# Gemv steps of the modulation on another engine around the first layer norm, and a table behind the last key activation

## The chip, the cores and the metric

One core of a Trainium2 chip runs the whole kernel in one launch. The metric is the device time of an execution in microseconds (us). An execution has five engines with a queue of instructions each: TensorE (PE, with its weight loads as PEld), VectorE (DVE), ScalarE (ACT), GpSimd (POOL) and SyncE (SP). SP issues nearly all transfers from memory. Each engine takes its instructions in a fixed order, and an instruction that waits holds up those behind it.

## The reference

All is fp32, with model width 2048, one sequence of 256 tokens, and weights of several hundred MB. Cut to what matters here:

```python
# two attention layers
for l in range(2):
    shift, scale, gate = split(silu(c) @ w_mod[l] + b_mod[l], 3)      # modulation: gemv
    h = x * (1 + scale) + shift
    if l == 0:
        y = diff_attention(h, ...)
    else:
        k, v, F = shared_kv(x, silu(c), w_kvmod, ...)   # hk = x*(1+scale')+shift'; hk @ w_kv
        y = forgetting_attention(h, w_q, w_out, k, v, F)
    x = layer_norm(ALPHA * x + gate * y, ln_g[l], ln_b[l])
# a state-space block
sh1, sc1, gt1, sh2, sc2, gt2 = split(silu(c2) @ w_mod2 + b_mod2, 6)   # gemv
h_ctx, h_lat = modulated rmsnorm of the context and of x
y = s5_mixer(h_ctx, h_lat, ...)      # linear recurrence over tokens, from the context's last state
x = x + gt1 * rmsnorm(y)
x = x + gt2 * rmsnorm(relu(modulate(rmsnorm(x), sh2, sc2) @ w1) ** 2 @ w2)
```

The modulation vectors are products of one activated vector with a wide matrix. They depend on no token, so they can be computed at any time before their use; what they cost is the reading of their weights and a pass of some engine over them.

## The kernel before

**Layout.** Activations lie transposed: `x` (tile `xres`) is 16 tiles of 128 features by 256 tokens. Each big product is done in three reduced-precision matmuls: a weight `w` is split into `wh` (cast by ScalarE, line 133) and `wl = w - wh` (VectorE, line 134), an activation likewise into H and L; then `hH*wh + hL*wh + hH*wl` (lines 162 to 164) are added in PSUM.

**The stream of weights.** `weights()` delivers the next block of 128 output features (1 MB in two loads). Each call also does two things in passing: one step of a background gemv, `bg()`, and as many steps of a side job, `step()`, as the cycle `steps` says.

**The background gemv.** `gemv()` works a modulation vector off in two halves of eight steps each. A step loads two 128x1024 tiles `graw` of 512 KB each from SP's queue; their pool `rg` has four buffers and is shared with the tile `wc` of the context. The step is used one call later (`LATE = 1`), in one of two ways. On "pe" it is eight matmuls, which the trace shows as 16 (an fp32 matmul shows as two), that add into a PSUM tile `g` (line 221). On "dve" it is two instructions `gacc += graw * c` (line 236). A half that has had a "dve" step is `open` until it is closed with matmuls of `gacc`. Which engine a step gets is a cycle of names set for each stage by `policy()`: `P_ON0` in the output projection of layer 0, `P_KV` in the keys' and values' stage, `P_QG` in the attention stage, `P_ON1` in the output projection of layer 1; `None` means no step. The jobs are done in the order of `JOBS`. The job `mc` has two outputs and runs on TensorE whatever the policy says. No step is ever dropped, so what one stage leaves out a later one has to do.

**The stages around the change.** `out_norm(0)` ends layer 0: 16 output blocks, the sums of the layer norm by matmuls, a chain of small VectorE instructions with an inverse root (`rsqrt`, lines 325 to 333), a broadcast of mean and root by TensorE (`lnb`, line 342), and then `norm(j)`: two VectorE instructions for each of 16 tiles (lines 1109 and 1110). `layer1()` makes the keys' activations from it: `affine_split` (lines 416 to 419) runs `norm(j)`, scales and casts on ScalarE (`u`, `kH`) and subtracts on VectorE (`kL`). The keys' stage then has 16 blocks (`mm_t`), the values' stage 16 half blocks (`mm_n`); the forget gate is computed behind the first block. A generator `s5_outputs_table` (`vgen`), with instructions on VectorE, ScalarE and TensorE and loads and stores on SP and POOL, is a side job of these 32 calls. The attention stage follows (32 calls), with the generator `ctx_states` as side job as soon as `mc` is done: it computes the state that the context leaves, in eight blocks of six levels each (lines 1332 to 1335). It runs on in `out_norm(1)`. `s5_mix` starts with the lines

```python
1364        self.bg_use(0)
1365        while self.open:
1366            self.bg(1, "dve")
1367            self.bg_use(0)
```

and then normalizes, modulates and transposes the tiles for the scan (lines 1407 to 1409), which is VectorE's.

**What sets the order.** The program is written in the order above, but a scheduler places each instruction on its engine's queue by a simulated timeline; the buffers of the pools set what a load has to wait for. `issue_after(ins)` is an extra edge that holds instructions behind `ins` on `ins`'s own engine, here VectorE; instructions on other engines are not held by it.

## Time and profile before

| | us |
|---|---|
| median of three timed executions | 2538.9 (2536.18 to 2539.73) |
| the profiled execution | 2539.89 |
| its span, first to last instruction | 2538.1 |
| TensorE busy | 2363.0 |
| VectorE busy | 1748.6 |
| ScalarE busy | 1191.3 |

The mean granted clock of TensorE is 0.953 of full speed. The durations further down are those of the profiled execution; its own time is 1.8 us more than its span, and 1.0 us more than the median. Names like `gacc<-graw` say what an instruction writes and reads. Times in the timeline count from the span's start.

### The profile page before, as it was taken

The numbers are of one execution on the slowest core, as the hardware profiler recorded it, in microseconds if no ns is written. First come the engines' busy times: TensorE is split into PE (matmuls) and PEld (weight loads), VectorE is DVE, ScalarE is ACT, GpSimd is POOL, SyncE is SP. The second block draws the span as 40 slices with busy tenths as digits, with TensorE's granted clock in tenths as the row PEclk, the third lists the DMA queues.
The fourth block names the chain that finished last, engine by engine and source line by source line (L and its number), as shares of the span: only waits on it lengthen the run. The fifth ranks groups of instructions, "written<-read, shape, count | busy, mean of one in ns | idle before, by whom it ended". The sixth has DMA issues, their size and how long they took to land.

```text
span 2538.1 us, 49977 instructions
## 1 busy us (share of the span) xinstructions
PE 2363.0 (93%) x19934; PEld 2042.3 (80%) x19934; DVE 1748.6 (69%) x3369; ACT 1191.3 (47%) x2069; POOL 96.4 (4%) x213
## 2 busy tenths in 40 slices
PE   5699999999989999999998569999899999999997
PEld 1289999999678888888896457898688888888885
DVE  3288778877785555788787896775864665665655
ACT  0455454445355556555443443544544443443442
POOL 0000000000001111000000000000000000000000
PEclk8599999999979999999998779999899999999998
DMA  9999999888869998888786357995356655556552
GB/s 324 337 337 321 323 328 340 304 286 300 281 210 346 327 338 295 286 273 295 235 295 245 116 182 271 359 318 194 117 186 192 189 189 189 185 188 190 189 185 94
DMA packets 195450, 644.78 MB, mean 254 GB/s; under 512 B 32624, under 2 KB 41072, under 8 KB 194832
## 3 DMA queue, kind: packets, MB, share of 16 engines
q1 hardware_dynamic: 187744, 620.47, 71.5%
q0 software_dynamic: 7472, 21.11, 2.1%
q8 instruction: 156, 2.56, 0.4%
q14 instruction: 78, 0.64, 0.1%
HBM read 615.80 MB, written 25.69 MB: 253 GB/s over the span
## 4 chain that ended last, share of the span: by engine, by line
PE 50%; issue 34%; DVE 7%; DMA 7%; ACT 2%; SPq 0%; POOL 0%; DVEq 0%; ACTq 0%; POOLq 0%
PE pj L162 10%; PE pj L163 10%; PE pj L164 10%; DMA graw<-in_w_mod 5%; PE g L221 3%; PE pjv L199 3%; PE pjv L200 2%; PE pjv L201 2%; PE ko L1451 2%; DVE scan_t L1407 1%; DVE S L1409 1%; DVE scan_t L1408 1%; PE y L1480 1%; PE st L369 1%; DVE gacc L236 1%
## 5 line engine op out<-in xcount | busy, mean ns | idle before, releaser
L134 DVE TENSOR_TENSOR wl<-w,wh 128x1024 fp32r<-128x1024 f32 x631 | 769.7, 1223 | 486.4 <-ACT wh L133 475.5
L133 ACT CAST wh<-w 128x1024 fp32r<-128x1024 f32 x632 | 658.1, 1048 | 741.0 <-PE pj L175 281.0
L175 PE MATMUL pj<-h,wh 128*128 128x512 f32 x1024 | 362.1, 399 | 5.7 <-DVE h L419 3.8
L175 PE MATMUL pj<-d,wh 128*128 128x512 f32 x1024 | 358.6, 396 | 0.0
L176 PE MATMUL pj<-h,wl 128*128 128x256 f32 x1024 | 287.0, 280 | 1.1 <-DVE wl L134 1.1
L176 PE MATMUL pj<-d,wl 128*128 128x256 f32 x1024 | 284.8, 279 | 0.0
L236 DVE SCALAR_TENSOR_TENSOR gacc<-graw,csilu,gacc 128x1024 f32<-128x1024 f32 x200 | 255.8, 1279 | 36.3 <-DMA graw<-in_w_mod 31.5
L175 PEld LDWEIGHTS pj<-h,wh 128*128 128x128 f32 x1024 | 193.6, 189 | 54.0 <-issue 3.9
L175 PEld LDWEIGHTS pj<-d,wh 128*128 128x128 f32 x1024 | 191.9, 188 | 47.5 <-PE pj L176 1.7
L162 PE MATMUL pj<-hH,wh 128*128 128x256 f32 x768 | 221.5, 289 | 5.2 <-ACT hH L418 4.0
L164 PE MATMUL pj<-hH,wl 128*128 128x256 f32 x768 | 221.4, 289 | 0.5 <-DVE wl L134 0.5
L163 PE MATMUL pj<-hL,wh 128*128 128x256 f32 x768 | 221.0, 288 | 0.0
L221 PE MATMUL g<-graw,czc 128*32 128x256 f32 x1840 | 169.5, 452 | 42.7 <-DMA graw<-in_w_mod 39.1
L176 PEld LDWEIGHTS pj<-h,wl 128*128 128x128 f32 x1024 | 194.2, 190 | 1.5 <-DVE wl L134 1.5
L176 PEld LDWEIGHTS pj<-d,wl 128*128 128x128 f32 x1024 | 192.8, 188 | 0.4
L162 PEld LDWEIGHTS pj<-hH,wh 128*128 128x128 f32 x768 | 148.8, 194 | 8.8 <-ACT hH L418 4.1
L164 PEld LDWEIGHTS pj<-hH,wl 128*128 128x128 f32 x768 | 148.5, 194 | 4.5 <-issue 3.3
L163 PEld LDWEIGHTS pj<-hL,wh 128*128 128x128 f32 x768 | 148.8, 194 | 3.8 <-issue 3.7
L162 PE MATMUL pj<-h1H,wh 128*128 128x256 f32 x512 | 146.3, 288 | 0.0
L163 PE MATMUL pj<-h1L,wh 128*128 128x256 f32 x512 | 145.9, 286 | 0.0
L164 PE MATMUL pj<-h1H,wl 128*128 128x256 f32 x512 | 145.1, 284 | 0.0
L221 PEld LDWEIGHTS g<-graw,czc 128*32 128x32 f32 x1840 | 48.8, 117 | 115.7 <-DMA graw<-in_w_mod 88.4
(475 smaller groups left out, 5067.6 us busy)
## 6 DMA issues: line engine op xcount, KB each, us to landing
graw<-in_w_mod SPq DMA_DIRECT2D x384, 512.0 KB, 5.8
w<-in_mlp_in SPq DMA_DIRECT2D x128, 512.0 KB, 3.7
w<-in_mlp_out SPq DMA_DIRECT2D x128, 512.0 KB, 3.7
w<-in_a_in SPq DMA_DIRECT2D x96, 512.0 KB, 6.1
graw<-in_w_kvmod SPq DMA_DIRECT2D x64, 512.0 KB, 6.0
w<-in_b_in SPq DMA_DIRECT2D x64, 512.0 KB, 5.6
w<-in_glu SPq DMA_DIRECT2D x56, 512.0 KB, 5.6
w<-in_a_v SPq DMA_DIRECT2D x32, 512.0 KB, 5.8
```

Of the source, the lines that this page charges most:

```text
L133: nc.scalar.copy(h, src)
L134: (eng or (nc.gpsimd if next(self.spl) else nc.vector)).tensor_sub(l, src, h)
L162: self.nc.tensor.matmul(ps, h, aH, start=kt == order[0] and not opened, stop=False)
L163: self.nc.tensor.matmul(ps, h, aL, start=False, stop=False)
L164: self.nc.tensor.matmul(ps, l, aH, start=False, stop=kt == order[-1] and last)
L175: self.nc.tensor.matmul(ps, h, view(aH, 0, [[T, 2], [1, T]]), start=kt == order[0], stop=False)
L176: self.nc.tensor.matmul(ps[:, 0], l, aH, start=False, stop=kt == order[-1])
L199: self.nc.tensor.matmul(ps[:, i], aH[:, s], h, start=half == 0 and i == 0 and k == 0, stop=False)
L200: self.nc.tensor.matmul(ps[:, i], aH[:, s], l, start=False, stop=False)
L201: self.nc.tensor.matmul(ps[:, i], aL[:, s], h, start=False, stop=half == 1 and i == 1 and k == 7)
L221: nc.tensor.matmul(st["g"][32 * q:32 * q + 32], self.cz[c][:, ch * 2 + s], raw[s][:, q * 256:q * 256 + 256], start=st["n"] == 0, stop=ch = ...
L236: nc.vector.scalar_tensor_tensor(acc, raw[s], cc, acc, op0=MUL, op1=ADD)
```

## The change

Five things. (1) `P_ON0` gives no gemv step in the last four of the 16 output blocks of layer 0: 9 steps rather than 12. (2) The six steps at the start of layer 1 are issued ahead of `affine_split` rather than behind it, and on TensorE; before they took the engine that the job's table names, VectorE. (3) `affine_split` returns its last subtraction, and the VectorE instructions of every side job are held behind that one until the end of the values' stage. (4) `vgen` starts at the second call, and every eighth call does two of its steps. (5) `P_KV` begins with TensorE.

```diff
--- before.py
+++ after.py
@@ -50,12 +50,13 @@
 KO_K = 12
 P_START = ("pe",)
 P_L0A = ('dve', 'pe')
-P_KV = ('dve', 'pe')
+P_KV = ('pe', 'dve')
+P_VT = (1, 1, 1, 1, 1, 1, 1, 2)
 P_QG = ('dve', 'dve', 'pe')
 P_W = ("pe",)
 P_GLU = ('dve',)
 P_MLP = ('dve', None, None)
-P_ON0 = ('dve', 'dve', 'dve', None)
+P_ON0 = ('dve', 'dve', 'dve', None) * 3 + (None,) * 4
 P_ON1 = ('pe', 'dve', None)
 BG_V = 2
 BG_W = 0
@@ -271,8 +272,9 @@
 
     def step(self):
 
-        while self.side and next(self.side[0], True):
-            self.side.pop(0)
+        with self.tc.issue_after(self.after) if self.after else nullcontext():
+            while self.side and next(self.side[0], True):
+                self.side.pop(0)
 
     def flush(self, job):
         while job in self.side:
@@ -416,7 +418,8 @@
             nc.scalar.activation(u, src(j), AF.Identity, scale=S[:, j:j + 1], bias=B[:, j:j + 1])
             aH, aL = dst(j)
             nc.scalar.copy(aH, u)
-            nc.vector.tensor_sub(aL, u, aH)
+            last = nc.vector.tensor_sub(aL, u, aH).ins
+        return last
 
     def pair(self, name):
         H, L = self.act_tile(F32R, name + "H"), self.act_tile(F32R, name + "L")
@@ -728,6 +731,7 @@
             self.steps = itertools.cycle((1,))
             self.open = False
             self.side = []
+            self.after = None
             self.x = xr.tile([128, KT, T], F32, name="xres")
             mod = lambda n: self.vt.tile([128, KT], F32, name=n)
             self.m0 = [mod(f"m0_{i}") for i in range(3)]
@@ -1119,8 +1123,8 @@
             self.bg_finish(n)
         S, B = self.small_bg("lk", V("lg0"), self.mk[1], V("lb0"), self.mk[0])
         k_ = self.pair("k")
-        self.affine_split(self.norm, S, B, k_)
-        self.bg(BG_K, E_K)
+        self.bg(BG_K, "pe")
+        self.after = self.affine_split(self.norm, S, B, k_)
         Fs = self.cp.tile([48, T], F32R, name="Fs")
         nid = self.cp.tile([48, 16], F32R, name="nid")
         FT = self.cp.tile([128, 2, 16], F32, name="FT")
@@ -1168,9 +1172,10 @@
         kT, v = [], []
         self.policy(P_KV, X_KV)
         vgen = self.s5_outputs_table(self.act.tile([128, 4096], F32, name="gen2_ws", tag="act"))
-        self.side.append(vgen)
         for j in range(32):
             if j == 1:
+                self.side.append(vgen)
+                self.steps = itertools.cycle(P_VT)
                 F = forget()
             if j == 3:
                 forget_t(F)
@@ -1189,6 +1194,8 @@
                         nc.scalar.copy(t, ps[:, :, h * 128:h * 128 + 128])
                         v.append(t)
         self.flush(vgen)
+        self.steps = itertools.cycle((1,))
+        self.after = None
         for i in (1, 0):
             self.bg_finish(f"m1_{i}")
         s1 = self.plus1("s1_1", self.m1[1])
```

Counted over the whole program, TensorE has 56 gemv matmuls more and VectorE 14 gacc instructions fewer; everything else is there as often as before. The lines of the changed kernel are up to seven higher than those of the kernel before (line 236 becomes 237, 419 becomes 421, 1109 and 1110 become 1113 and 1114).

By the stages, the gemv's steps come to stand as follows: start of layer 1, 6 on VectorE before, 6 on TensorE now; keys and values, 3 on VectorE and 29 on TensorE before, 4 and 28 now; attention, 18 and 14 before, 16 and 16 now; output projection of layer 1, 11 both times; the loop at the start of `s5_mix`, 3 before, 6 now, all on VectorE. `ctx_states` begins one head later.

VectorE's queue among the first keys, before. `gacc` is the gemv, `vprod` and `gen_ws` are the table, the other three the norm and the keys:

```order
L1110 TENSOR_TENSOR xres<-xres,lnb 128x256
L1109 TENSOR_TENSOR xres<-xres,lnb 128x256
L419 TENSOR_TENSOR kL<-u,kH 128x256
L236 SCALAR_TENSOR_TENSOR gacc<-graw,csilu,gacc 128x1024
L1110 TENSOR_TENSOR xres<-xres,lnb 128x256
L1109 TENSOR_TENSOR xres<-xres,lnb 128x256
L419 TENSOR_TENSOR kL<-u,kH 128x256
L553 TENSOR_TENSOR vprod<-gen_ws 128x512
L554 TENSOR_TENSOR vprod<-gen_ws 128x512
L236 SCALAR_TENSOR_TENSOR gacc<-graw,csilu,gacc 128x1024
L1110 TENSOR_TENSOR xres<-xres,lnb 128x256
L1109 TENSOR_TENSOR xres<-xres,lnb 128x256
```

The same place now:

```order
L421 TENSOR_TENSOR kL<-u,kH 128x256
L1114 TENSOR_TENSOR xres<-xres,lnb 128x256
L1113 TENSOR_TENSOR xres<-xres,lnb 128x256
L421 TENSOR_TENSOR kL<-u,kH 128x256
L1114 TENSOR_TENSOR xres<-xres,lnb 128x256
L1113 TENSOR_TENSOR xres<-xres,lnb 128x256
L421 TENSOR_TENSOR kL<-u,kH 128x256
L1114 TENSOR_TENSOR xres<-xres,lnb 128x256
L1113 TENSOR_TENSOR xres<-xres,lnb 128x256
L421 TENSOR_TENSOR kL<-u,kH 128x256
L1114 TENSOR_TENSOR xres<-xres,lnb 128x256
L1113 TENSOR_TENSOR xres<-xres,lnb 128x256
```

The gemv's and the table's instructions have left this stretch; the three instructions of a key tile follow each other.

VectorE's queue at the end of the norm's first inverse root and behind it, at the start of `s5_mix`, before. `ry` and `rq` are the root, `rc` leads to the second root (the rms norm's):

```order
L1093 COPY mr1_16129<-ry_16136 128x2
L1102 TENSOR_TENSOR rc_16153<-rc_16153,ry_16136 128x2
L1103 SCALAR_TENSOR_TENSOR rc_16153<-ra_16152,rc_16153 128x2
L1104 TENSOR_TENSOR rc_16153<-rc_16153,ry_16136 128x2
L1105 TENSOR_SCALAR rc_16153<-rc_16153,ms_14546 128x2
L236 SCALAR_TENSOR_TENSOR gacc_15739<-graw_16242,csilu_147,gacc_15739 128x1024
L1106 TENSOR_SCALAR rc_16153<-rc_16153 128x2
L1109 TENSOR_TENSOR xres_99<-xres_99,lnb_16147 128x256
L325 TENSOR_SCALAR ry_16163<-rc_16153 128x2
L1110 TENSOR_TENSOR xres_99<-xres_99,lnb_16147 128x256
L1109 TENSOR_TENSOR xres_99<-xres_99,lnb_16147 128x256
L327 TENSOR_TENSOR rq_16164<-ry_16163 128x2
```

A piece of the same chain now, between the sums and the first root; `ctx_ws` is the last block of the context's states:

```order
L237 SCALAR_TENSOR_TENSOR gacc_15989<-graw_16258,csilu_147,gacc_15989 128x1024
L1342 TENSOR_TENSOR ctx_ws_12029<-ctx_ws_12029 128x16x32
L327 TENSOR_SCALAR ry_16115<-lv_16111 128x2
L237 SCALAR_TENSOR_TENSOR gacc_15989<-graw_16260,csilu_147,gacc_15989 128x1024
L1339 TENSOR_TENSOR ctx_ws_12029<-ctx_ws_12029 128x512
L1340 TENSOR_TENSOR ctx_ws_12029<-ctx_ws_12029 128x512
L329 TENSOR_TENSOR rq_16116<-ry_16115 128x2
L1102 SCALAR_TENSOR_TENSOR ra_16131<-sums_16105,mr1_16108 128x2
L1341 TENSOR_TENSOR ctx_ws_12029<-ctx_ws_12029 128x512
L237 SCALAR_TENSOR_TENSOR gacc_15989<-graw_16264,csilu_147,gacc_15989 128x1024
L330 SCALAR_TENSOR_TENSOR rq_16116<-rq_16116,lv_16111 128x2
L1103 SCALAR_TENSOR_TENSOR rc_16132<-lq_16110,ms_14483,ra_16131 128x2
```

Before, one `gacc` stands between the sums and the second root, and now there are eleven, with the context's 512-element instructions between them.

TensorE's queue at the end of the same norm, before. `st` and `sums` are the norm's sums, `lnb` the broadcast of mean and root; the broadcast `rb` of the second root comes two rows further on:

```order
L221 MATMUL g_15549<-graw_16037,czc2_154 32x256 x4
L221 MATMUL g_15549<-graw_16039,czc2_154 32x256 x4
L369 MATMUL st_15403<-zsq_16104,mw_14538 3x256
L369 MATMUL st_15403<-xres_99,mw_14538 3x256
L369 MATMUL st_15403<-zsq_16109,mw_14538 3x256
L369 MATMUL st_15403<-xres_99,mw_14538 3x256
L369 MATMUL st_15403<-zsq_16114,mw_14538 3x256
L369 MATMUL st_15403<-xres_99,mw_14538 3x256
L369 MATMUL st_15403<-zsq_16119,mw_14538 3x256
L364 MATMUL st_15403<-zero_137 128x256
L379 MATMUL sums_16126<-sel_ln_160,sumst_16123 128x6 x2
L342 MATMUL lnb_16147<-idn_130,mr1_16129 128x128 x4
```

And now:

```order
L371 MATMUL st_15375<-zsq_16098,mw_14475 3x256
L366 MATMUL st_15375<-zero_137 128x256
L698 MATMUL inc_16155<-uctx_15395,wc_16028 64x64
L698 MATMUL inc_16156<-uctx_15395,wc_16028 64x64 x2
L381 MATMUL sums_16105<-sel_ln_160,sumst_16102 128x6 x2
L344 MATMUL lnb_16126<-idn_130,mr1_16108 128x128 x4
L344 MATMUL rb_16152<-idn_130,ry_16142 128x128 x2
L222 MATMUL g_16243<-graw_15985,czc2_154 32x256 x4
L222 MATMUL g_16243<-graw_15987,czc2_154 32x256 x4
L246 MATMUL g_16243<-gacc_15989,one32_139 32x256 x4
```

The gemv matmuls of the half step on TensorE stood ahead of the sums, and stand now behind `rb`. Until they have run, their two `graw` buffers of four are not free.

## Rows read from the trace of the kernel before

**Rows 1.** The page, busy time and share of the span by engine.
```profile
PE 2363.0 (93%) x19934; PEld 2042.3 (80%) x19934; DVE 1748.6 (69%) x3369; ACT 1191.3 (47%) x2069; POOL 96.4 (4%) x213
```

**Rows 2.** Windows by stage: us, busy us (instructions) per engine, clock, DMA share, GB/s.
```profile
686.00:735.00 49.00, 35.88 (x175) 29.23 (x176) 44.23 (x92) 24.89 (x51) 2.50 (x8) 0.65 0.66 210
735.00:965.00 230.00, 230.00 (x2404) 200.29 (x2406) 134.35 (x189) 127.62 (x242) 38.82 (x86) 1.00 0.92 321
...
985.00:1240.00 255.00, 251.61 (x2572) 224.17 (x2571) 196.28 (x340) 141.86 (x295) 5.97 (x12) 1.00 0.84 287
...
1352.00:1375.00 23.00, 21.96 (x226) 16.59 (x224) 17.32 (x39) 5.42 (x14) 0.00 (x0) 1.00 0.90 334
1375.00:1490.00 115.00, 60.75 (x1448) 48.45 (x1450) 106.81 (x550) 52.32 (x111) 1.39 (x4) 0.70 0.40 139
```

**Rows 3.** Timeline of VectorE, 685 to 702: start, us, instruction.
```profile
693.29 1.28 DVE L236 SCALAR_TENSOR_TENSOR gacc<-graw,csilu,gacc 128x1024 f32<-128x1024 f32 x1
694.50 0.15 DVE L1089 TENSOR_TENSOR lq<-mr 128x2 f32<-128x2 f32 x1
...
698.14 0.42 DVE L1109 TENSOR_TENSOR xres<-xres,lnb 128x256 f32<-128x256 f32 x1 [1.31 <-PE lnb L342]
```

**Rows 4.** VectorE's groups, 698 to 738: shapes, count, busy us, mean ns, idle.
```profile
L236 DVE SCALAR_TENSOR_TENSOR gacc<-graw,csilu,gacc 128x1024 f32<-128x1024 f32 x7 | 8.9, 1275 | 0.0
...
L134 DVE TENSOR_TENSOR wl<-w,wh 128x1024 fp32r<-128x1024 f32 x4 | 4.9, 1217 | 0.0
L553 DVE TENSOR_TENSOR vprod<-gen_ws 128x512 f32<-128x512 f32 x4 | 2.7, 681 | 0.0
```

**Rows 5.** Tile kL: duration in ns (min/median/max), first and last start.
```profile
L419 DVE TENSOR_TENSOR kL<-u,kH x16: 414/415/425, 701.1 to 734.6; 128x256 fp32r<-128x256 f32 x16
```

**Rows 6.** TensorE's groups, 698 to 738.
```profile
L163 PE MATMUL pj<-kL,wh 128*128 128x256 f32 x54 | 19.8, 374 | 4.8 <-DVE kL L419 4.8
L164 PE MATMUL pj<-kH,wl 128*128 128x256 f32 x52 | 18.2, 355 | 1.2 <-DVE wl L134 1.2
L162 PE MATMUL pj<-kH,wh 128*128 128x256 f32 x55 | 15.7, 359 | 2.9 <-ACT kH L418 2.9
```

**Rows 7.** Windows within the ramp.
```profile
698.00:706.00 8.00, 5.51 (x22) 4.70 (x21) 7.83 (x17) 4.22 (x10) 0.00 (x0) 0.50 0.77 234
...
710.00:723.00 13.00, 10.48 (x45) 9.39 (x45) 13.00 (x27) 6.76 (x13) 0.55 (x1) 0.50 0.63 198
```

**Rows 8.** Timeline of TensorE, 740 to 748.
```profile
745.18 0.28 PE L164 MATMUL pj<-kH,wl 128*128 128x256 f32 x1
745.30 0.28 PE L162 MATMUL pj<-kH,wh 128*128 128x256 f32 x1
...
745.75 1.07 PE L221 MATMUL g<-graw,czc 128*32 128x256 f32 x16
```

**Rows 9.** Timeline of VectorE, 1350 to 1408.
```profile
1357.83 0.68 DVE L1333 TENSOR_TENSOR ctx_ws<-ctx_ws 128x512 f32<-128x512 f32 x1
...
1362.01 1.28 DVE L236 SCALAR_TENSOR_TENSOR gacc<-graw,csilu,gacc 128x1024 f32<-128x1024 f32 x1 [2.16 <-DMA graw<-in_w_mod]
...
1374.22 0.16 DVE L1087 TENSOR_SCALAR mr<-sums 128x2 f32<-128x2 f32 x1 [0.37 <-PE sums L379]
...
1378.08 1.28 DVE L236 SCALAR_TENSOR_TENSOR gacc<-graw,csilu,gacc 128x1024 f32<-128x1024 f32 x1
...
1381.89 0.16 DVE L333 SCALAR_TENSOR_TENSOR ry<-rq,ry 128x2 f32<-128x2 f32 x1
...
1406.41 0.23 DVE L1408 TENSOR_TENSOR scan_t<-scan_t,S 128x64 f32<-128x64 f32 x1
```

**Rows 10.** DMA issues, 700 to 725: count, KB, median us to landing.
```profile
graw<-in_w_mod SPq DMA_DIRECT2D x7, 512.0 KB, 3.9
```

**Rows 11.** DMA issues, 1370 to 1392.
```profile
graw<-in_w_mod SPq DMA_DIRECT2D x5, 512.0 KB, 8.6
```

## The prediction

> **What bounds the kernel now.** I read the page's first section, then busy time by stage, and, for the two stages that the change reaches, the timelines of VectorE and TensorE. TensorE is busy for 93% of the span and VectorE for 69% [rows 1], but these are averages. By stage [rows 2] the reader is to see that TensorE is full in the keys' and values' stage (230.0 of 230 us at full clock) and in the attention stage (251.61 of 255), so that there a VectorE instruction costs nothing and a TensorE instruction its whole length. Two stretches are VectorE's. One is the ramp behind the first layer norm, 686 to 735: VectorE 44.23 of 49, TensorE 35.88 at a mean clock of 0.65. The other begins at 1375: VectorE 106.81 of 115, TensorE 60.75. The change lightens the first and, as the order of the instructions tells, loads the head of the second.
>
> **The ramp (place A): what is taken away.** From the first norm instruction at 698.14 [rows 3] to the end of the last kL at 734.6 + 0.41 = 735.0 [rows 5], VectorE works 36.9 us almost without a gap. Consecutive instructions overlap a little: the gacc at 693.29 is 1.28 long and the next row starts 1.21 behind it. So I price each by its length less 0.08: 0.335 us for kL (0.415 [rows 5]) and for the two norm instructions of the same size, 1.2 for gacc, 1.14 for a wl split, 0.6 for a 512-element table instruction [rows 4]. 48 x 0.335 = 16.1 for the norm and the keys, 7 x 1.2 = 8.4 for gacc, 4 x 1.14 = 4.6 for the weights, and 12 table instructions, of which one group of four is shown, 7.2. The sum is 36.3, which agrees with 36.9. In the changed order six of the seven gaccs are gone from there and the table stands behind the last kL: 16.1 + 1.2 + 4.6 = 21.9 us, 15 less.
>
> The statistics of the norm, ahead of it, also hold a gacc: it runs at 693.29 and the chain goes on only at 694.50 [rows 3]. Without it, and with the gaccs ahead of the sums gone too, I take 1 to 2.3 us off the start, so the first norm at about 696.5 and the last kL at 718 to 719, some 16 us earlier.
>
> **The ramp: what TensorE makes of it.** TensorE runs 54 + 52 + 55 = 161 matmuls of the keys between 698 and 738 [rows 6]; at the pitch of full clock (0.12 us, the first two of [rows 8]) they are 19.3 us. So it loses 40 - 19.3 = 20 us there: 8.9 waiting for kL, kH and wl, the first key's kH among them [rows 6], and the rest by the clock. The granted clock was 0.50, 1.2 GHz, from 698 to 706 with TensorE busy 5.51 of 8, and 0.50 again from 710 to 723 [rows 7]. After the change a kL comes every 21.9 / 16 = 1.4 us rather than 2.3, so TensorE has more to do at a stretch. It also has six gemv steps, of which three stand before the first key matmul and three among them; a step is 16 matmuls, 1.07 us at full clock [rows 8]. I take: start of key matmuls at 698; 19.3 of matmuls; 3 us of gemv steps behind the start; 3 us for the stretch that still runs at half clock; 0.5 idle: 723.8 against 738, a gain of 14. The bounds are 6 and 15: at 6 most of the ramp stays at 1.2 GHz (twice the pitch on 161 matmuls costs 19 more in full, and the 21.9 us in which the keys come hide more than half of it), at 15 TensorE follows VectorE without a loss. Above 16 there is no room, since kL itself comes no earlier.
>
> **Place A, the smaller parts.** The steps of the first modulation in the keys' stage now begin with TensorE, and 28 gemv steps in the stage run there rather than 29: -1 us. Three steps less in the out-projection (9 for 12): VectorE isn't what binds there, 0. The table moves later in a stage where VectorE has 134.35 of 230 [rows 2]; that hides it. If its tail reaches beyond the stage it stands among the first activations of the attention stage: 0 to +3, taken 1. The attention stage takes 16 TensorE steps for 14, in a stage where TensorE is full: +2. Sum of A: -14 - 1 + 1 + 2 = -12, with ends -2 and -14.
>
> **Start of S5 (place B): what is added.** Since three steps fewer were done early, and no step was taken away in all, three more are left when the out-projection of layer 1 ends. There the code finishes whatever half is open on VectorE: before 3 steps were left (6 loads of 512 KB), now 6 (12 loads), each with a gacc of 1.28 us. The state table of the context also starts one head later and ends later. On VectorE's order all this stands inside the two inverse roots of the second norm, on which S5 waits. Before, from the first instruction of the statistics at 1374.22 to the end of the second root at 1381.89 + 0.16 = 1382.05, there are 7.8 us, with one gacc (1378.08) [rows 9]. Now the order has 11 gaccs and the last block of the context's table in that chain: 10 more gaccs at 1.2 are 12.0; 8 table instructions of 512 elements at 0.68 - 0.08 (the row at 1357.83) are 4.8; four of 256 at 0.33 and eleven smaller ones add 2.4, less some 2 us of the short latencies that these hide. That is 17 more, by VectorE's own work alone, from the moment when the sums arrive.
>
> **Place B: the loads.** Four buffers take the loads. Two of them hold the half step that TensorE will do, and on TensorE's order it now stands behind the instruction that waits for the second root. So the twelve loads go through two buffers: a load is issued when the gacc before it on its buffer has ended. From issue to landing a graw took 3.9 us in the ramp with few others [rows 10] and 8.6 at 1370 to 1392, where many were in flight [rows 11]; before, VectorE waited 2.16 us for one at 1362.01 [rows 9]. Two loads each 3.9 + 1.28 = 5.2 us, six rounds, are 31 us; the first is issued at about 1370, so the last gacc ends at 1401 to 1402, and the second root some 1.5 us behind it, 1403: +21. By VectorE's work alone it would be 1375 + 25 = 1400: +18. The Trainium skill (DMA: Bandwidth & Descriptors, Anatomy of one DMA — SWDGE (gpsimd) path) gives a fit of 2.0 us plus bytes over 436 GB/s, 3.2 us for such a load, measured on another path; by it six rounds are 27 and VectorE's work would decide, +18. No run here shows 3.2. I take +20; nothing behind it makes up for it, since VectorE is at 106.81 of 115 from 1375 to 1490 [rows 2]; the scan begins at 1406.41 [rows 9] and shifts with it. Ends: +10 (the last waits of the old order, up to 5 us before the scan, take part, and the first gaccs fall before the sums) and +25 (loads at 5 to 6 us).
>
> **The sum.** -12 + 20 = +8. The profiled execution took 2539.89 us, so 2547.9; the median of the timed runs stands 1.0 below it, at 2538.9, and so 2547.
>
> **The rivals.**
> - *Only the added work counts at S5's start, and the ramp pays in full.* If the loads land early and VectorE does most gaccs before the sums, the added work is six gaccs (7.2) and some of the table (2.4), less the 5.7 us that VectorE stands idle from 1352 to 1375 (17.32 of 23 busy [rows 2]): +4. With -14 for A: 2538.9 - 10 = 2529. The idle time speaks for it; against it that VectorE's order is fixed, with eleven gaccs behind the sums, and that two of four buffers are held. It decides if the second root ends within some 15 us of the sums, where it was 7.8. Chance 0.13; not slower.
> - *The two places cancel.* The ramp gives its utmost (A -14), S5's start costs 13 to 15: 2539. Each end is within its bounds. Chance 0.18.
> - *TensorE stays at half clock.* The gemv matmuls now stand among the keys' matmuls, and they need loads; where one is late the array idles and the clock stays at 0.50 as it did from 710 to 723. The ramp gives only 6 (A -4), S5's start costs 20: 2555. For it: the clock fell before after a single wait; against it: the loads are issued in the out-projection. Chance 0.14.
> - *The table isn't held where it is meant to be.* The edge is on VectorE's queue alone, so its ScalarE copies and SP loads run early and could stand before keys' work: 1 or 2 us of the gain. That is 2549, and its chance is in the forecast's.
>
> **How the numbers follow.** The forecast with +1 to +13 has 0.55; the others as given. What a measurement of this kernel can tell from no change is 0.2%, 5.1 us. Slower by more: 0.85 of 0.55, and 0.14, together 0.61. Same: 0.15 of 0.55 and 0.9 of 0.18, 0.24. Faster: the rest, 0.15. The range runs from 2530, which takes in most of the first rival, to 2558, which takes in the half clock. The likeliest case's own is 2540 to 2554.
>
> **What would show it.** Right: VectorE from the first norm to the last kL in 22 to 24 us, without gacc but one, and TensorE past its 161 matmuls 12 to 15 us sooner; eleven gaccs between the statistics of the second norm and its second root, with waits for graw; the scan's first row about 20 us late against the same point of the ramp. Wrong: the second root within 15 us of the sums, or a clock of 0.50 through the ramp.

## The result and the profile after

| us | before | after |
|---|---|---|
| median of four timed executions | 2539.3 (2536.2 to 2541.7) | 2560.9 (2556.1 to 2565.0) |
| the profiled execution, its span | 2539.9, 2538.1 | 2559.4, 2557.6 |

The ratio is 1.0083, with an interval of 1.0068 to 1.0098: slower, by more than twice what was forecast. The marks below are differences of the first or last start of a tile (`sums`, `kL`, `h1L`, `scan_t`, `xy`, the last being the result of the gated unit behind the scan). They divide the span, so the last column adds up to the 19.5 us that the span has grown.

| from one mark to the next, us | before | after | change |
|---|---|---|---|
| start to the first norm's sums | 692.2 | 688.8 | -3.4 |
| to the last key matmul | 149.7 | 137.0 | -12.7 |
| to the last value matmul | 122.3 | 122.4 | +0.1 |
| to the first attention matmul | 2.2 | 3.9 | +1.7 |
| to the last attention matmul | 269.7 | 281.7 | +12.0 |
| to the second norm's sums | 137.8 | 138.3 | +0.5 |
| to the scan's first row | 32.5 | 55.5 | +23.0 |
| to the end of the span | 1131.7 | 1130.0 | -1.7 |

The ramp and the keys gave nearly what was forecast (the last key matmul comes 16.1 us earlier, for 15), and S5's start took a little more. The 12 us in the attention stage are what the forecast did not have. The page's first line, which answers to [rows 1], shows nothing of it: TensorE works 2.3 us more and VectorE 16.7 less.

```profile
PE 2365.3 (92%) x20046; PEld 2033.2 (79%) x20046; DVE 1731.9 (68%) x3355; ACT 1190.5 (47%) x2069; POOL 96.8 (4%) x213
```

The windows by stage answer to [rows 2] and [rows 7], with the same columns:

```profile
686.00:735.00 49.00, 44.97 (x360) 33.38 (x355) 34.15 (x82) 27.50 (x56) 1.11 (x2) 0.90 0.77 253
735.00:950.00 215.00, 211.57 (x2143) 185.07 (x2146) 132.79 (x181) 118.70 (x223) 36.39 (x78) 1.00 0.88 312
952.00:1234.00 282.00, 274.72 (x2749) 237.60 (x2745) 198.13 (x348) 155.22 (x332) 11.59 (x25) 0.99 0.86 292
...
1372.00:1403.00 31.00, 2.25 (x11) 1.68 (x11) 24.83 (x61) 0.64 (x2) 0.00 (x0) 0.57 0.64 188
...
698.00:706.00 8.00, 7.26 (x51) 5.12 (x44) 5.54 (x17) 5.00 (x13) 0.00 (x0) 0.64 0.91 322
...
710.00:723.00 13.00, 13.00 (x110) 9.56 (x109) 7.85 (x15) 7.81 (x13) 0.57 (x1) 1.00 0.79 245
```

In the ramp TensorE's busy time by its clock is 44.97 x 0.90 = 40.5 us of full speed, where it was 35.88 x 0.65 = 23.3. The product is an estimate, since the two figures are means over the window. The 17 us more are the 3.4 by which the sums came earlier and some 14 that were idle or at half clock. The stretch 710 to 723, at 0.50 before, is at 1.00 with TensorE busy throughout. The row at 1372 is the new hole: 31 us in which TensorE does 2.25 us of work and VectorE 24.83.

VectorE's timeline in the ramp, which answers to [rows 3] (start, us, instruction, idle time ahead of it and what ended it):

```profile
694.53 0.42 DVE L1113 TENSOR_TENSOR xres<-xres,lnb 128x256 f32<-128x256 f32 x1 [2.57 <-PE lnb L344]
...
705.85 0.43 DVE L421 TENSOR_TENSOR kL<-u,kH 128x256 fp32r<-128x256 f32 x1 [2.42 <-ACT kH L420]
...
714.41 1.23 DVE L135 TENSOR_TENSOR wl<-w,wh 128x1024 fp32r<-128x1024 f32 x1 [3.07 <-ACT wh L134]
...
721.15 1.28 DVE L237 SCALAR_TENSOR_TENSOR gacc<-graw,csilu,gacc 128x1024 f32<-128x1024 f32 x1 [2.05 <-ACT gacc L235]
...
723.49 0.42 DVE L421 TENSOR_TENSOR kL<-u,kH 128x256 fp32r<-128x256 f32 x1
```

From the first norm instruction to the end of the last kL (694.53 to 723.91) it takes 29.4 us, 36.9 before. It has one gacc, and three waits for ScalarE (2.42, 3.07, 2.05) that were not there before: with its own work gone, VectorE is no longer what bounds the ramp (e7_nohold below bears this out).

TensorE's groups from the sums to 728.6 answer to [rows 6]: 162 key matmuls are done by then, with 112 / 16 = 7 gemv steps.

```profile
L164 PE MATMUL pj<-kL,wh 128*128 128x256 f32 x54 | 15.6, 305 | 0.0
L165 PE MATMUL pj<-kH,wl 128*128 128x256 f32 x54 | 15.0, 291 | 0.0
L163 PE MATMUL pj<-kH,wh 128*128 128x256 f32 x54 | 13.5, 308 | 0.0
L222 PE MATMUL g<-graw,czc 128*32 128x256 f32 x112 | 11.9, 487 | 3.1 <-DMA graw<-in_w_mod 3.1
```

At S5's start the timeline of VectorE answers to [rows 9]; eleven gaccs stand between the first and the last root, of which three rows are shown:

```profile
1372.36 0.16 DVE L1091 TENSOR_SCALAR mr<-sums 128x2 f32<-128x2 f32 x1 [5.03 <-PE sums L381]
...
1378.74 1.29 DVE L237 SCALAR_TENSOR_TENSOR gacc<-graw,csilu,gacc 128x1024 f32<-128x1024 f32 x1 [0.63 <-DMA graw<-in_w_mod]
...
1398.53 1.28 DVE L237 SCALAR_TENSOR_TENSOR gacc<-graw,csilu,gacc 128x1024 f32<-128x1024 f32 x1 [0.76 <-DMA graw<-in_w_mod]
...
1401.45 1.28 DVE L237 SCALAR_TENSOR_TENSOR gacc<-graw,csilu,gacc 128x1024 f32<-128x1024 f32 x1 [1.10 <-DMA graw<-in_w_mod]
...
1404.66 0.16 DVE L335 SCALAR_TENSOR_TENSOR ry<-rq,ry 128x2 f32<-128x2 f32 x1
...
1427.58 0.23 DVE L1415 TENSOR_TENSOR scan_t<-scan_t,S 128x64 f32<-128x64 f32 x1
```

The waits of 1372 to 1403 (us in total, times, longest), and the loads of that stretch, which answer to [rows 11]:

```profile
PE lnb L344 <- DVE rc L1106: 18.7, 1, 18.7
DVE gacc L237 <- DMA graw<-in_w_mod: 5.8, 8, 1.1
```

```profile
graw<-in_w_mod SPq DMA_DIRECT2D x11, 512.0 KB, 4.4
```

The chain from `mr` to the end of the second root is 32.5 us (1372.36 to 1404.82), 7.8 before. The waits for loads are 5.8 of it, and the rest is VectorE at work on what was put in between.

### The profile page after: what moved, and what is told of

It reads as the page before. It is cut to its first block, busy times and chain, and to the rows that moved or that the text cites. A ratio compares the mean times of both kernels' runs of the same rounds, so it can differ in the third digit from the quotient of the medians.

```text
span 2557.6 us, 50138 instructions
## 1 busy us (share of the span) xinstructions
PE 2365.3 (92%) x20046; PEld 2033.2 (79%) x20046; DVE 1731.9 (68%) x3355; ACT 1190.5 (47%) x2069; POOL 96.8 (4%) x213
## 4 chain that ended last, share of the span: by engine, by line
PE 79%; DVE 8%; DMA 7%; ACT 3%; issue 3%; SPq 0%; POOL 0%; DVEq 0%; ACTq 0%
PE pj L176 18%; PE pj L163 10%; PE pj L165 10%; PE pj L164 10%; PE pj L177 9%; DMA graw<-in_w_mod 6%; PE g L222 4%; PE pjv L201 2%; PE pjv L202 2%; PE pjv L200 2%; PE ko L1458 2%; DVE scan_t L1414 1%; DVE wl L135 1%; DVE S L1416 1%; DVE scan_t L1415 1%
## 5 line engine op out<-in xcount | busy, mean ns | idle before, releaser
L237 DVE SCALAR_TENSOR_TENSOR gacc<-graw,csilu,gacc 128x1024 f32<-128x1024 f32 x186 | 237.9, 1279 | 49.5 <-DMA graw<-in_w_mod 39.6
L222 PE MATMUL g<-graw,czc 128*32 128x256 f32 x1952 | 182.9, 459 | 49.1 <-DMA graw<-in_w_mod 46.1
```

Of the source, the lines that this page charges most:

```text
L222: nc.tensor.matmul(st["g"][32 * q:32 * q + 32], self.cz[c][:, ch * 2 + s], raw[s][:, q * 256:q * 256 + 256], start=st["n"] == 0, stop=ch = ...
L237: nc.vector.scalar_tensor_tensor(acc, raw[s], cc, acc, op0=MUL, op1=ADD)
```

## The experiments

The table gives each kernel's ratio to the kernel before, and six stretches of its profiled execution. "Early" and "late" are the attention stage's first 12 weight blocks (heads 0 to 5) and its other 20; they are divided at the first `h1L` matmul of block 13, in every kernel, and add up to the stage. With "early" stand the gemv steps that TensorE ran there (rows of `g<-graw` in the trace, over 16). "Projection" is layer 1's output projection, to the second norm's sums. Each stretch comes from one execution, and executions of one kernel differ by up to 17 us (e6_vt1: 2548.7 to 2565.6), so a few us in one stretch of one kernel are not shown by themselves.

| | ratio (interval) | sums to last key | early: us / steps | late | projection | sums to scan | scan to xy |
|---|---|---|---|---|---|---|---|
| before | 1 | 149.7 | 103.4 / 8 | 166.3 | 137.8 | 32.5 | 370.6 |
| after | 1.0083 (1.0068 to 1.0098) | 137.0 | 113.2 / 15 | 168.5 | 138.3 | 55.5 | 369.8 |
| e1_on0_back | 0.9919 (0.9902 to 0.9935) | 143.8 | 104.6 / 10 | 167.5 | 134.7 | 31.1 | 359.5 |
| e3_on0_only | 1.0044 (1.0028 to 1.0059) | 139.1 | 105.3 / 12.5 | 166.9 | 143.8 | 56.0 | 360.1 |
| e4_six_pe | 0.9935 (0.9921 to 0.9949) | 141.9 | 101.5 / 8 | 166.5 | 133.8 | 31.7 | 369.2 |
| e5_hold | 0.9902 (0.9886 to 0.9919) | 145.3 | 100.1 / 8 | 168.2 | 133.1 | 31.4 | 360.5 |
| e9_kv_back | 0.9938 (0.9921 to 0.9954) | 143.0 | 106.0 / 10 | 164.6 | 134.2 | 31.9 | 365.0 |
| e7_nohold | 1.0082 (1.0067 to 1.0097) | 134.5 | 113.2 / 15 | 166.1 | 136.7 | 55.5 | 375.3 |
| e12_on1_all | 1.0016 (1.0005 to 1.0028) | 136.0 | 113.0 / 15 | 166.2 | 139.8 | 36.1 | 370.6 |
| e8_qg_pe | 0.9955 (0.9939 to 0.9972) | 149.7 | 103.5 / 9 | 166.7 | 131.8 | 31.8 | 366.9 |
| e13_early_pe | 0.9992 (0.9982 to 1.0002) | 150.9 | 107.4 / 12 | 165.5 | 133.1 | 30.9 | 367.9 |
| e6_vt1 | 1.0064 (1.0048 to 1.0081) | 138.1 | 105.5 / 11 | 167.1 | 144.0 | 54.9 | 366.8 |
| e14_hold_qg | 0.9954 (0.9938 to 0.9970) | 144.9 | 100.9 / 9 | 168.4 | 132.9 | 31.0 | 367.9 |

**The three steps of layer 0's output projection.** First the changed kernel with this one edit undone, then the kernel before with this one edit made.

```diff
e1_on0_back, against the changed kernel:
-P_ON0 = ('dve', 'dve', 'dve', None) * 3 + (None,) * 4
+P_ON0 = ('dve', 'dve', 'dve', None)
```

> The changed kernel with the twelve gemv steps of the first output projection again (three steps more there, all else as changed). Theory: the start of S5 costs the changed kernel 23 us because three more steps are left there, so with them done early the second root comes about 8 us behind the sums again and the kernel takes 2538 to 2541 us: the keys' ramp gains about 12 and the attention stage gives 9 to 12 back. Rival 1: the attention stage's 12 us belong to the three steps that were pushed back, too; then both are gone and the time is 2526 to 2530. Rival 2: the loss at the start of S5 comes from the context's table that starts a head later; then the chain stays over 20 us long and the time is over 2555.

Measured: 2521.4 us, 20 less than before and 40 less than after. The chain of S5's start is back at 31.1, so the three deferred steps are its whole cost. The attention stage falls too, from 281.7 to 272.1, as rival 1 says: 9.6 of its 12 us go with the same edit. Some 10 us of the gain belong to neither: they lie between scan and xy (359.5), where no edit of the change is; with the changed kernel's length there it would be 2531.7.

```diff
e3_on0_only, against the kernel before:
-P_ON0 = ('dve', 'dve', 'dve', None)
+P_ON0 = ('dve', 'dve', 'dve', None) * 3 + (None,) * 4
```

> The kernel before, with nothing changed but the three gemv steps left out in the last four blocks of the first output projection. Theory: the loss at the start of S5 comes whole (eleven gaccs between the sums and the second root, the chain 30 us long instead of 8), less 2 us for the gaccs gone from the first norm's statistics: 2558 to 2564 us. Rival: the loss needs the other parts, too (the buffers held, the later table); then 2540 to 2550.

Measured: 2552.6. VectorE's timeline shows the same chain, with eleven gaccs in it:

```profile
1371.59 0.16 DVE L1087 TENSOR_SCALAR mr<-sums 128x2 f32<-128x2 f32 x1 [5.03 <-PE sums L379]
...
1402.57 0.16 DVE L333 SCALAR_TENSOR_TENSOR ry<-rq,ry 128x2 f32<-128x2 f32 x1
...
1427.29 0.23 DVE L1408 TENSOR_TENSOR scan_t<-scan_t,S 128x64 f32<-128x64 f32 x1
```

So this edit alone makes the chain (56.0 from sums to scan). The span grows by less than the chain, 14.1 us: the keys gave 10.6 and the scan-to-xy stretch 10.5 (360.1). The projection took 6.0 more (143.8), most of it one wait for VectorE in its middle (`p` is a sum for the norm, over the blocks so far):

```profile
PE p L369 <- DVE xres L1069: 5.0, 1, 5.0
```

The edit also takes gacc out of the ramp by itself: none is left between the first norm and the last kL (727.9), and the last key comes 10.6 us sooner against the sums. Part of what I put down to the move of the six steps could therefore be had without it.

The smaller `P_ON0` costs time ahead of the chain, too. The attention stage and the projection together (early, late and projection in the table) take 416 to 420 us in the five kernels that have it, and 401 to 408 in the eight that don't. e3 alone adds 8 us there, and e1 takes 13 away. The number of TensorE steps does not sort them: over the two stages e3 has 24.5 and e8_qg_pe 25, at 416.0 and 402.0.

**The other parts alone.** The six steps, and then the hold of the table, each in the kernel before.

```diff
e4_six_pe, against the kernel before:
+        self.bg(BG_K, "pe")
         self.affine_split(self.norm, S, B, k_)
-        self.bg(BG_K, E_K)
```

> The kernel before, with nothing changed but the six gemv steps at the start of layer 1, which go to TensorE and ahead of the keys' activations. Theory: VectorE's ramp loses 7 gaccs (8 us), TensorE gets 6 us of work of which the ramp's idle time hides most, but matmuls that slip behind the ramp cost their whole length: 2533 to 2538 us. Rival: all six slip into full stages, gain 8 less 6, and 2537 to 2540.

```diff
e5_hold, against the kernel before (with step(), affine_split and the resets as in the change):
+P_VT = (1, 1, 1, 1, 1, 1, 1, 2)
-        self.affine_split(self.norm, S, B, k_)
+        self.after = self.affine_split(self.norm, S, B, k_)
         self.bg(BG_K, E_K)
-        self.side.append(vgen)
         for j in range(32):
             if j == 1:
+                self.side.append(vgen)
+                self.steps = itertools.cycle(P_VT)
```

> The kernel before, with nothing changed but the table: it is held behind the last key activation and starts one call later, with a double step every eighth call. Theory: 7 us of VectorE's work leave the ramp, TensorE gains about as much there, and the table's tail costs 1 to 3 us between the values' stage and the attention stage: 2532 to 2537 us. Rival: the gaccs alone set the ramp, so nothing is gained and the tail costs 2: 2539 to 2542.

Measured: 2523.5 and 2516.8, both more gain than expected. The keys' end comes 7.8 and 4.4 us sooner against the sums, and the attention stage takes that back in neither (268.0, 268.3). The scan begins at 1390.2 and 1393.8, 16 and 13 sooner than before; some 4 us of each lie in layer 1's output projection (133.8 and 133.1 for 137.8). There the kernel before has one wait near its head that is 1.2 and 0.7 us in these two:

```profile
PE pj L162 <- ACT oH L1241: 3.9, 1, 3.9
```

e5_hold is 10 us shorter between scan and xy as well, where ScalarE waits less for the weights of the gated unit. The rows are of the kernel before and of e5_hold, between scan and xy:

```profile
ACT wh L133 <- DMA w<-in_glu: 24.4, 9, 13.8
```

```profile
ACT wh L134 <- DMA w<-in_glu: 11.4, 8, 2.9
```

The stretch is 359.5 to 360.5 in three kernels and 365.0 to 375.3 in the others, and nothing in the edits sorts them. What sets it stays open. e5_hold has the lowest median of all the kernels here; its interval overlaps with that of e1.

```diff
e9_kv_back, against the changed kernel:
-P_KV = ('pe', 'dve')
+P_KV = ('dve', 'pe')
-P_ON0 = ('dve', 'dve', 'dve', None) * 3 + (None,) * 4
+P_ON0 = ('dve', 'dve', 'dve', None)
```

> The changed kernel with the twelve steps of the first output projection and with the old order of engines in the keys' stage: only the six TensorE steps and the hold of the table are left of the change. By themselves they brought the first row of the scan 16 and 13 us earlier than in the kernel before. Theory: both fill the same idle time of TensorE in the ramp, so together they bring 15 to 19, not 29. Rival: they add; 25 to 29 us earlier. In the second experiment of this kind (with the new order of engines) it was 7 earlier; if it is that again, the order of engines isn't the reason.

Measured: 2524.1. In the ramp (-6.7) the six steps and the hold together gain no more than the six steps alone (-7.8), and the scan begins 14.7 us sooner than before, for 16 and 13 by themselves. They do not add, as expected; that both empty the same stretch of VectorE is the likely reason, not shown. e1 differs from this kernel by the order of engines alone. There the scan began 7.3 us sooner than before; the other 7 us are spread over several stretches, at most 2.6 in one, and the intervals of the two totals overlap. So nothing here shows a price for that order.

```diff
e7_nohold, against the changed kernel:
-        self.after = self.affine_split(self.norm, S, B, k_)
+        self.affine_split(self.norm, S, B, k_)
```

> The changed kernel without the hold: the table's VectorE instructions are free to go among the key activations again, all else as changed. Theory: with the gaccs gone VectorE has room in the ramp, so 7 us of table there let the last kL come about 6 us later, but TensorE, which is busy with gemv steps, loses only 2 to 4: 2559 to 2566 us. Rival: the hold is worth what it was by itself on the kernel before (14 us after its gain in a stretch that no edit touches is taken off): 2572 to 2577.

Measured: 2561.6, the changed kernel's time. The last kL starts at 729.6 rather than 723.5, so the table does come back into VectorE's ramp, which takes 36.1 us again, with three gaccs; but the last key matmul comes 2.5 us sooner against the sums, not later. With fewer gaccs the end of kL isn't what TensorE waits for, and the hold is worth nothing there.

**Where the deferred steps go.** The changed kernel with more steps in layer 1's output projection, which takes them out of S5's start.

```diff
e12_on1_all, against the changed kernel:
-P_ON1 = ('pe', 'dve', None)
+P_ON1 = ('pe', 'dve')
```

> The changed kernel with a gemv step in every block of the second output projection (16 rather than 11), so that the open half is closed before its end. Theory: what costs 23 us at the start of S5 is that the steps stand between the sums and the second root; five more steps in the projection, where TensorE is full, cost 2 to 5 us there, and from the last sums to the first row of the scan it takes 34 to 40 us instead of 55.5: 2540 to 2548 us in all. Rival: the 12 loads are what costs; then the projection grows by 15 us or more, since it moves 262 GB/s already, and the time stays over 2553.

Measured: 2545.4. The chain is back to 11.3 us (7.8 before), and the projection is 1.5 us longer than in the changed kernel (139.8). VectorE's timeline, and its gacc group in the projection, 16 gaccs with 19.8 us of waiting for loads that cost the stage next to nothing:

```profile
1374.12 0.15 DVE L1091 TENSOR_SCALAR mr<-sums 128x2 f32<-128x2 f32 x1
...
1385.30 0.16 DVE L335 SCALAR_TENSOR_TENSOR ry<-rq,ry 128x2 f32<-128x2 f32 x1
...
1409.24 0.23 DVE L1415 TENSOR_TENSOR scan_t<-scan_t,S 128x64 f32<-128x64 f32 x1
```

```profile
L237 DVE SCALAR_TENSOR_TENSOR gacc<-graw,csilu,gacc 128x1024 f32<-128x1024 f32 x16 | 20.5, 1281 | 19.8 <-DMA graw<-in_w_mod 19.8
```

It is 15 us better than the changed kernel and still 6 worse than before: the attention stage keeps most of its excess (279.2).

**The attention stage.** First more steps on TensorE throughout the stage, then twelve of them at its head.

```diff
e8_qg_pe, against the kernel before:
-P_QG = ('dve', 'dve', 'pe')
+P_QG = ('dve', 'pe')
```

> The kernel before, with every second instead of every third gemv step of the attention stage on TensorE: four steps more of 16 matmuls there. Theory: TensorE is full in this stage and each step costs its length, 1.07 us: the attention stage takes 4 to 5 us more (269.7 before), and the second output projection 1. Rival: the stage's length is set by the chain of the softmax on ScalarE and VectorE, and the steps go into waits: 0 to 1 us more.

Measured: the stage takes 270.3 us, 0.6 more for four steps more, as the rival says. That a step costs TensorE its length there falls, for steps spread like this. What differs from the changed kernel is the place, too: e8 has 9 steps among the early heads (8 before), the changed kernel 15.

```diff
e13_early_pe, against the kernel before:
-P_QG = ('dve', 'dve', 'pe')
+P_QG = ('pe',) * 12 + ('dve', 'dve', 'pe') * 7
```

> The kernel before, with the gemv steps of the first six heads of the attention stage all on TensorE and the others as they were: four steps more, 18 in all, as many as where every second one went there, but all of them early. There the stage grew by 0.6 us (269.7 to 270.3). Theory: in the first six heads TensorE sets the pace (99.6 us with 7 steps there, 112.7 with 15 in the changed kernel, 1.1 to 1.6 us a step), in the last ten the heads' own chain does: heads 0 to 5 take 104 to 106 us here, the stage 274 to 276. Rival: a step costs nothing anywhere in the stage, and the changed kernel's 12 us have another cause: heads 0 to 5 stay at 99 to 101 us.

Measured: 107.4 us for the early heads, 4.0 more for four steps more, some 1.0 each; the stage takes 3.2 more, and the total is that of before. The two figures in the expectation, 99.6 and 112.7, end at different instructions: divided at the same one they are 103.4 and 113.2, and the changed kernel's seven steps more come with 1.4 us each. At e13's price the seven steps would be 7 of the 9.8 us by which the early heads grew, so some 3 have another cause. The gemv's group among the early heads, in before, after and e13_early_pe (x128 and x192 are 8 and 12 steps; x244 is 15 and the last rows of the one ahead):

```profile
L221 PE MATMUL g<-graw,czc 128*32 128x256 f32 x128 | 12.2, 388 | 0.0
```

```profile
L222 PE MATMUL g<-graw,czc 128*32 128x256 f32 x244 | 19.3, 390 | 0.8 <-DMA graw<-in_w_mod 0.8
```

```profile
L221 PE MATMUL g<-graw,czc 128*32 128x256 f32 x192 | 17.5, 387 | 0.0
```

Over all the kernels in the table the early heads take 100 to 104 us with 8 or 9 steps, 105 to 107 with 10 to 12.5, and 113 with 15. The late ones take 164.6 to 168.5, in no order by their steps. The whole stage takes 268 to 273 with 14 to 19.5 steps (ten kernels) and 279 to 282 with 21 (three): the excess is not in proportion to the steps.

```diff
e6_vt1, against the changed kernel:
-P_VT = (1, 1, 1, 1, 1, 1, 1, 2)
+P_VT = (1,)
```

> The changed kernel without the double step of the table at every eighth call. On TensorE's queue 18.5 gemv steps rather than 23 then stand in the attention stage, and 4.5 more in the keys' and values'. Theory: a step costs its length in either place, so what the first six heads gain (112.7 to some 107 us) the keys and values lose: the second norm's sums come within 2 us of the changed kernel's, counted from the first norm's. Rival: the steps find idle time in the keys' ramp; then the sums come 4 to 5 us earlier. The start of S5 is as in the changed kernel, 55 us from the sums to the scan, in both.

Measured: 2557.2, an interval that overlaps with the changed kernel's. The attention stage takes 272.7 us, 9.0 less (18 steps for 21, of them 11 early for 15). So its excess needs the table's double step as well as the three deferred steps of e1; without the one or the other 2.4 and 3.0 us of it are left. Against the first sums the stage ends 7 us sooner, and the projection takes 5.7 more, most of it one wait of `p` for `xres`, 4.9 us, as in e3.

```diff
e14_hold_qg, against the kernel before: the edits of e5_hold, and
-P_QG = ('dve', 'dve', 'pe')
+P_QG = ('dve', 'pe')
```

> The kernel before, with the table held behind the last key activation and with every second gemv step of the attention stage on TensorE: the two edits that by themselves brought the most without a new wait. By itself the first took 2516.8 us and the second 2528.4 (before 2540 to 2542). Theory: they touch different stages and add, except for what each gained behind the scan's start, which isn't theirs: the first row of the scan comes 18 to 22 us earlier than before (13 and 8 by themselves), 2505 to 2518 us in all. Rival: the gain of the second is part of the first; 12 to 14 earlier.

Measured: 2530.1, slower than e5_hold. The scan begins 12.0 us sooner than before, as the rival says. The gains don't add up: each alone shortens layer 1's output projection from 137.8 us to 133.1 (hold) and 131.8 (steps), and together to 132.9. The wait of 3.9 us near its head can be lost only once.

## Why the prediction was right in direction and short in size

- **S5's start, right.** +20 forecast, +23.0 measured; e3 makes it alone and e1 takes it away alone. Order, count and place of the gaccs were as read. The loads landed in 4.4 us at the median where I took 3.9, and two buffers at 4.4 + 1.28 us a round are one gacc every 2.8; eleven stand between 1372.94 and 1402.73, every 2.7. The 3.2 us of the Trainium skill's fit (DMA: Bandwidth & Descriptors, Anatomy of one DMA — SWDGE (gpsimd) path) were not met.
- **The ramp, right in sum.** Forecast -14 for it and -1 for the rest of the keys; the last key came 12.7 sooner against the sums (16.1 against the span's start), and the values' stage did not change. The working was off in two places. VectorE needed 29.4 us rather than 21.9, since it then waits for ScalarE. And the 161 matmuls were through at some 728.5 rather than 723.8, 9.5 us sooner than before and not 12 to 15, with seven gemv steps ahead of them; the stage got that back behind the ramp. That the sum came out nearly right is in part luck, since the two errors were made up for behind the ramp. e7 and e3 show that the hold adds nothing to this, and that the smaller `P_ON0` would have cleared VectorE's ramp of gacc alone.
- **The attention stage, wrong.** "The attention stage takes 16 TensorE steps for 14, in a stage where TensorE is full: +2" is the step that failed: it measured +12.0. Both of its factors, the count and the price, were wrong. I counted steps by the policy of each stage: by the trace TensorE ran 14 of them there before and 21 now. The ramp and the keys went from 12 to 14.5, the values, with the few us behind them, from 17 to 14.5, and what the change added to TensorE, 7 steps, came out of the values' end among the early heads. Counted from the last value matmul on, TensorE runs 23 steps to the end of the stage, for 15 before; it takes its queue in order, so this could be read beforehand. And I priced the stage by steps alone. From each matmul's start to the next one's, the gemv takes only 4.2 us more there and its closing 1.5 less; the tail of the table takes 1.6 more, the context's matmuls 1.7, and the stage's own projections 5.7, with the same 1,532 matmuls. TensorE's idle time grew by 3.9 us (busy 266.31 of 269.70 before, 274.52 of 281.80 now). By e1 and e6 the excess needs the three deferred steps and the table's double step together; what holds the projections' matmuls up is open. Where the steps were held shows at the end of a half, whose next step stands behind `gr` on TensorE's queue; before, and after:

```profile
888.01 1.07 PE L221 MATMUL g<-graw,czc 128*32 128x256 f32 x16
...
897.99 0.61 PE L251 MATMUL gr<-sel,gs 128*128 128x8 f32 x4
...
898.53 1.07 PE L221 MATMUL g<-graw,czc 128*32 128x256 f32 x16
```

```profile
918.17 0.64 PE L222 MATMUL g<-graw,czc 128*32 128x256 f32 x8
...
942.08 0.61 PE L252 MATMUL gr<-sel,gs 128*128 128x8 f32 x4
...
950.25 1.91 PE L222 MATMUL g<-graw,czc 128*32 128x256 f32 x32
```

  From the last step of a half to the first of the next it was 10.5 us, and is 32.1 here. Why `gr` was put so late is open; I don't know which instruction the scheduler waited for.
- **What a step costs there** was wrong as well, but not always: four more among the early heads cost 3.2 us in the stage, not far from their length of 1.07 each (e13), and four more spread over it 0.6 (e8). What tells early from late heads I can't show.
- **The smaller terms.** The sums came 3.4 us sooner, which I had only inside the ramp; the transition cost 1.7 for 1.
- **The rivals.** None took place. The clock did not stay at 0.50, and the second root was 32.5 us behind the sums, not within 15.

From +8 to the span's +19.5: attention 10, S5 3, the keys 2, transition and projection 1, less 3.4 for the sums and 1.7 behind the scan.

## What to carry to other kernels

Work that is taken out of one stage and has to be done all the same is to be followed, in the order of the instructions, to the place where something first waits for it: here three steps, six gaccs of 1.28 us, became 23 us, because they came to stand inside a chain of 0.2 us instructions that a whole engine waits for. Count what lands in a stage by the queue, not by the policy that issues it, and don't take the count times a length for the price: seven steps were 4 of the 12 us. And try the parts alone: of this change the six steps gained 0.65%, the hold 0.98% (10 of its 25 us in a stretch that no edit explains), the cut in the first projection lost 0.44%, and all together lost 0.83%. The whole without the cut gained 0.81%, again with 10 us in that stretch.

## What was not expected of the hardware

A TensorE that reads as busy nearly all the time was not full. These are the attention stages of before, e8_qg_pe and after, in the columns of the windows: busy 266.31 of 269.70, 267.83 of 270.30 and 274.52 of 281.80, for 2722, 2786 and 2748 matmuls. The 64 rows more of e8_qg_pe took 0.6 us.

```profile
966.40:1236.10 269.70, 266.31 (x2722) 236.31 (x2721) 203.11 (x357) 156.68 (x329) 9.21 (x18) 1.00 0.83 284
```

```profile
964.50:1234.80 270.30, 267.83 (x2786) 237.68 (x2785) 194.86 (x352) 157.28 (x330) 10.13 (x18) 1.00 0.82 283
```

```profile
952.10:1233.90 281.80, 274.52 (x2748) 237.49 (x2745) 198.03 (x348) 155.03 (x332) 11.59 (x25) 0.99 0.86 292
```

A matmul's row is 0.28 us long, and rows follow each other by 0.12 where nothing holds them [rows 8], so a gap shorter than 0.16 behind a row doesn't show as idle. The Trainium skill says the like (Perfetto Trace Analysis, Tensor Engine Instruction (MATMUL, LD_WEIGHTS)): the end of a matmul's row is an estimate from its size, not an observation. The trace agrees: a row is longer than the distance to the next one. Four steps more in e8_qg_pe cost 0.6 us in a stage whose busy share reads 98% or more. What room is left in such a stage is told by adding a step, not by the busy share.
